# A two-layer hybrid RWKV / attention / Fourier block: the tile framework's scheduler with another machine model

## The chip, the core and the metric

The kernel runs on one core of one Trainium2 chip. The metric is the device time of one execution, in microseconds (us). The core has a matrix engine (PE, with its weight loads shown apart as PEld), a vector engine (DVE), a scalar engine (ACT), a general engine (POOL) and an engine that only issues transfers here (SP). Each engine takes its instructions strictly in the order that the built program gives it, and waits on semaphores for the others.

## The reference, cut to what matters

Two layers; 512 latent tokens and 256 context tokens, width 1024.

```python
for l in range(DEPTH):                       # 2 layers, the second without the context's output
    a  = modulate(rms_norm(h, ...), m[0], m[1]);  ac = the same for the context
    u  = a @ w_in[l]                         # one projection for three mixers and their gates
    # 1. RWKV-7, both directions, a state of 64x64 per head:
    #    S = S*w_t + (S @ -kk_t) b_t + v_t k_t ;  y_t = S r_t      (context first, then latent)
    # 2. windowed attention with the context as extra keys      3. 2-D Fourier mixing
    mix = (g_r*(y_r@wb_r) + g_a*(y_a@wb_a) + g_f*(y_f@wb_f)) @ w_out
    h   = h + m[2]*rms_norm(mix)
    h   = h + m[5]*rms_norm(conv_ffn(modulate(rms_norm(h), m[3], m[4])))
```

All matrix products are in float32 precision; the kernel makes each of three products of a rounded high part and a low rest.

## The kernel before, in words

**Products.** `gemm3` (lines 171 to 179) makes a product of 128-row blocks: for each block of the contraction three matmuls, on lines 177 (high by high), 178 (high by low) and 179 (low by high). A moving operand is 512 columns wide (latent tokens) or 256 (context tokens); in the ConvFFN of layer 0 it is 384. Weights come by `wload`: a transfer, a rounding on ACT (line 106) and the rest on POOL or DVE (line 118, `wl`).

**Stages of a layer.** First the projections that the RWKV mixer needs (`mix`, columns `COLS`). Then the RWKV chain: the tokens are cut into six windows of 128 (two of the context, four of the latent stream), each window into two chunks of 64, forward and backward direction together. For each window `wkv_features` makes decays, keys and products (matmuls on lines 814 and 864, DVE on 825 to 870), `wkv_inverse` inverts triangular blocks (matmuls 938 to 974, DVE 917 to 977), and for each chunk `wkv_prep` transposes (lines 987 and 997) and `wkv_step` advances the state (matmuls 1021 to 1052). One chunk needs the state of the chunk before: this is a chain over twelve steps, called the chain below. `rwkv_readout` follows (lines 1081 to 1107). Then Fourier mixing (lines 1298, 1305), attention (1222 to 1268), merging, the output projection, and the ConvFFN (`ffn`, the accumulation of its second product on line 604).

**What lies beside the chain.** The chain stands in blocks `with tc.high_priority()`. Beside it the kernel writes products that don't depend on it: eight column blocks for attention and Fourier (tile `stg`) and, by the generator `fill`, twelve blocks of gate columns (`AHEAD = 12`, written to `gd` through `sg`). Their accumulators have the PSUM tag `mm`. After that `self.banks(...)` hands the PSUM banks on, and the gates that are left take the tag `x`: they can't begin ahead of the chain's last use of its banks. These matmuls on lines 177 to 179 ahead of that point are called the fillers here.

**What sets the order.** No order is written out: the tile framework records the instructions of `run` in program order, each with its dependencies and a priority (program order, the high-priority blocks first). On leaving `tile.TileContext` (line 1804) its scheduler plays the program on a model of the machine: an engine that falls free in that model takes the ready instruction of the highest priority. The row in which the model took them is the order that stands in the program for each engine, for good. The model decides nothing else: which instructions there are, their operands and buffers' depth are the kernel's.

## Time and profile before

| | |
|---|---|
| time, median of 3 runs | 2510.15 us (2508.0 to 2512.45) |
| the profiled execution's own time | 2513.85 us |
| its span on the core | 2511.9 us, 43604 instructions |
| PE busy / PEld busy | 91% / 77% of the span |
| DVE / ACT / POOL busy | 75% / 42% / 38% |
| mean granted PE clock | 0.965 |

Busy time is the union of an engine's instructions. A matmul's shown duration reaches to the modelled end of its way through the array, and the next one starts long before that; how dense a stretch is shows in the distance of starts. The granted clock is a share of full speed: 1.0 is 2.4 GHz, 0.5 is 1.2 GHz, values between are means over a stretch. Lines are those of the kernel before. By the trace the stages of layer 0 are: projections up to about 148 us, the chain from there to 439, its readout to 473, Fourier mixing to 548, attention and merging to about 880, ConvFFN to about 1440; in layer 1 the chain runs from 1539 to 1812, its readout to 1833, and the ConvFFN from about 2135 to the end.

### The profile page before, as it was taken

The page shows a single profiled execution, that of the slowest core. Times are in us where ns is not written, and L with a number is a line of the kernel's source. Part 1 is how long each engine was busy: PE and PEld are TensorE (multiplying, and loading weights), DVE is VectorE, ACT ScalarE, POOL GpSimd, SP SyncE. Part 2 cuts the span into 40 slices and gives each one's busy share as a digit, 9 for nine tenths or more (in the row PEclk, how much of TensorE's full clock was granted, in tenths as well). Part 3 has the DMA queues.
Part 4 walks back from the last instruction along what each step waited for, and adds up shares of the span by engine and source line. Part 5 has one row for each costly group of instructions (what it writes and reads, how often), then busy time and mean ns, then how long its engine had stood idle before and what let it go on. Part 6 is the DMA issues. An engine that isn't in the chain of part 4 may idle for free. (4 is left out here: it accounts for less than half of the span.)

```text
span 2511.9 us, 43604 instructions
## 1 busy us (share of the span) xinstructions
PE 2293.3 (91%) x16612; PEld 1923.1 (77%) x16612; DVE 1889.0 (75%) x3458; ACT 1052.8 (42%) x2153; POOL 965.1 (38%) x965
## 2 busy tenths in 40 slices
PE   7878999999999979999999989889889997899997
PEld 4757777887777768898898777667667776888886
DVE  4967777838866587778778854888667857989988
ACT  3234343335434444343333544435345434544443
POOL 4443322023332363333333544343224424644453
PEclk9989989999999989999999999899999998999999
DMA  7611111644334322222222322112275643322321
GB/s 241 190 51 47 57 37 46 204 146 122 118 122 125 104 67 65 63 72 68 64 69 66 122 93 63 54 59 61 76 211 149 195 128 113 117 88 85 98 89 59
DMA packets 284529, 251.36 MB, mean 100 GB/s; under 512 B 14524, under 2 KB 241300, under 8 KB 284320
## 3 DMA queue, kind: packets, MB, share of 16 engines
q1 hardware_dynamic: 284320, 248.58, 32.0%
q8 instruction: 131, 2.15, 0.4%
q14 instruction: 78, 0.64, 0.1%
HBM read 221.23 MB, written 27.29 MB: 99 GB/s over the span
## 5 line engine op out<-in xcount | busy, mean ns | idle before, releaser
L177 PE MATMUL mm<-at,wh 128*128 128x256 f32 (+2 forms) x1968 | 661.8, 337 | 14.4 <-DVE v L614 7.0
L178 PE MATMUL mm<-at,wh 128*128 128x256 f32 (+2 forms) x1968 | 660.5, 336 | 12.8 <-POOL at L118 7.3
L179 PE MATMUL mm<-at,wl 128*128 128x256 f32 (+2 forms) x1968 | 659.7, 336 | 8.2 <-DVE wl L118 5.9
L118 POOL TENSOR_TENSOR wl<-wr,wh 128x512 fp32r<-128x512 f32 (+1 forms) x248 | 341.8, 1385 | 466.2 <-ACT wh L106 444.0
L177 PEld LDWEIGHTS mm<-at,wh 128*128 128x128 f32 x1968 | 380.8, 194 | 46.9 <-issue 5.6
L178 PEld LDWEIGHTS mm<-at,wh 128*128 128x128 f32 x1968 | 381.1, 194 | 43.4 <-POOL at L118 10.0
L179 PEld LDWEIGHTS mm<-at,wl 128*128 128x128 f32 x1968 | 380.9, 194 | 34.4 <-DVE wl L118 8.9
L106 ACT ACTIVATE wh<-wr 128x512 fp32r<-128x512 f32 (+1 forms) x342 | 204.9, 605 | 235.2 <-PE mm L178 141.3
L118 DVE TENSOR_TENSOR wl<-ws,wh 128x512 fp32r<-128x512 f32 x176 | 166.8, 949 | 65.6 <-ACT wh L106 65.6
L177 PE MATMUL x<-dh,hid 128*128 128x512 f32 x440 | 178.0, 405 | 29.8 <-DVE acc L604 27.7
L295 DVE SCALAR_TENSOR_TENSOR ma<-mw,s,ma 128x256 f32<-128x256 f32 x336 | 187.3, 597 | 11.0 <-DMA mw<-in_mod_w 8.2
L179 PE MATMUL x<-dh,hid 128*128 128x512 f32 x440 | 173.3, 395 | 1.0 <-DVE hid L118 1.0
L178 PE MATMUL x<-dl,hid 128*128 128x512 f32 x440 | 173.2, 394 | 0.0
L604 DVE TENSOR_TENSOR acc<-x,acc 128x512 f32<-128x512 f32 x200 | 134.4, 682 | 24.2 <-PE x L179 23.7
L118 POOL TENSOR_TENSOR dl<-dr,dh 128x1024 fp32r<-128x1024 f32 x44 | 112.2, 2549 | 83.9 <-ACT dh L106 83.9
L106 ACT ACTIVATE wh<-ws 128x512 fp32r<-128x512 f32 x170 | 103.7, 623 | 84.9 <-PE mm L178 70.5
L177 PEld LDWEIGHTS x<-dh,hid 128*128 128x128 f32 x440 | 83.3, 189 | 56.4 <-DVE acc L604 38.6
L154 POOL TENSOR_TENSOR ws<-wr,wr 128x512 f32<-128x512 f32 x42 | 66.4, 1580 | 139.5 <-DVE wl L118 136.9
L178 PE MATMUL x<-at,wh 128*128 128x512 f32 (+2 forms) x312 | 114.4, 367 | 5.0 <-POOL at L118 3.1
L177 PE MATMUL x<-at,wh 128*128 128x512 f32 (+2 forms) x312 | 114.7, 368 | 0.9 <-DVE wh L114 0.7
L106 ACT ACTIVATE P<-P,st 128x513 f32<-128x513 f32 (+5 forms) x120 | 86.0, 722 | 69.8 <-DVE P L1234 58.6
L154 POOL TENSOR_TENSOR ws<-ws,wr 128x512 f32<-128x512 f32 x42 | 62.8, 1495 | 132.5 <-DVE wl L118 75.0
(490 smaller groups left out, 4859.0 us busy)
## 6 DMA issues: line engine op xcount, KB each, us to landing
mw<-in_mod_w SPq DMA_DIRECT2D x96, 512.0 KB, 4.1
wr<-in_ffn_up SPq DMA_DIRECT2D x176, 256.0 KB, 3.1
wr<-in_w_in SPq DMA_DIRECT2D x164, 256.0 KB, 3.0
dr<-in_ffn_down SPq DMA_DIRECT2D x44, 512.0 KB, 3.3
gd<-sg SPq DMA_DIRECT2D x32, 256.0 KB, 2.0
wraw<-in_w_out SPq DMA_DIRECT2D x32, 256.0 KB, 3.7
hd<-h SPq DMA_DIRECT2D x32, 256.0 KB, 2.4
h<-hd SPq DMA_DIRECT2D x28, 256.0 KB, 6.7
```

Of the source, the lines that this page charges most:

```text
L106: return self.nc.scalar.activation(out, in_, func, **kw)
L118: e.tensor_tensor(lo, full, hi.bitcast(F32), ALU.subtract)
L154: e.tensor_tensor(raw[m], raw[x], raw[y], op)
L177: mm(ps, lhsT=lh, rhs=rh, start=first and k == 0, stop=False)
L178: mm(ps, lhsT=lh, rhs=rl, start=False, stop=False)
L179: mm(ps, lhsT=ll, rhs=rh, start=False, stop=last and k == nk - 1)
L295: nc.vector.scalar_tensor_tensor(acc[s], mw[:, k % 4], v, acc[s], ALU.mult, ALU.add)
L604: nc.vector.tensor_tensor(acc[i][:, cs], ps, acc[i][:, cs], ALU.add)
```

## The change

One argument. The scheduler plays the program on the framework's timeline simulator and no longer on its simple machine model.

```diff
-    with tile.TileContext(nc) as tc:
+    with tile.TileContext(nc, schedule_with_timeline_sim=True) as tc:
         Kern(tc, I, out).run()
```

The instructions are the same on PE (13680), DVE, POOL and SP; ACT has three table loads fewer. Their order differs on all five engines. Three places follow, each in the program before and in the changed one. In a row the tiles carry their buffer numbers: `x_588` is the PSUM tile of an inverse, `mm_...` the accumulator of a filler, `y_...` that of a step.

PE, layer 0, at the inverse of the chain's fourth window (line 938 is its first matmul). Before:

```order
L178 MATMUL mm_760_4834<-at_70_289,wh_754_4799 128x256
L179 MATMUL mm_760_4834<-at_69_288,wl_755_4800 128x256
L938 MATMUL x_588_3521<-iv_586_3517,MR_491_2911 32x16 x32
L177 MATMUL mm_760_4834<-at_71_290,wh_754_4799 128x256
L178 MATMUL mm_760_4834<-at_72_291,wh_754_4799 128x256
L179 MATMUL mm_760_4834<-at_71_290,wl_755_4800 128x256
L177 MATMUL mm_760_4834<-at_73_292,wh_757_4805 128x256
L178 MATMUL mm_760_4834<-at_74_293,wh_757_4805 128x256
L179 MATMUL mm_760_4834<-at_73_292,wl_758_4806 128x256
L944 MATMUL x_588_3521<-Ps_587_3520,TTt_585_3516 32x16 x16
L948 MATMUL x_588_3521<-TTt_585_3516,Ps_587_3520 16x16 x32
```

The same place in the changed program:

```order
L864 MATMUL x_578_3463<-W11_567_3414,BK_575_3442 128x128 x4
L938 MATMUL x_588_3521<-iv_586_3517,MR_491_2911 32x16 x32
L944 MATMUL x_588_3521<-Ps_587_3520,TTt_585_3516 32x16 x16
L948 MATMUL x_588_3521<-TTt_585_3516,Ps_587_3520 16x16 x32
L967 MATMUL x_590_3610<-iv_586_3517,MR_491_2911 32x32 x16
L987 MATMUL x_591_3647<-ident_2_61,vs__502_2950 128x128 x2
L987 MATMUL x_591_3647<-ident_2_61,vs__515_3008 128x128 x2
L974 MATMUL x_590_3610<-TTt_585_3516,Pb_589_3609 32x32 x16
```

The fillers that stood between the chain's matmuls here now stand ahead of this place. Counted from the start of the program, the fillers ahead of a point of the chain on PE are:

| point of the chain (layer 0: first four rows) | before | changed |
|---|---|---|
| first matmul of the first window's features (line 814) | 451 | 605 |
| first matmul of the first inverse (line 938) | 605 | 916 |
| first matmul of the fourth step (line 1021, `y_488`) | 732 | 1392 |
| last step (`y_697`) | 1111 | 1392 |
| layer 1: first inverse | 5829 | 6000 |
| layer 1: third step (`y_3206`) | 5879 | 6168 |
| layer 1: last step | 6168 | 6168 |

PE, layer 1, at the inverse of the chain's fourth window. Before:

```order
L864 MATMUL x_3307_17356<-W11_3296_17307,BK_3304_17335 128x128 x4
L178 MATMUL mm_3504_18758<-at_2843_14637,wh_3499_18748 128x512
L179 MATMUL mm_3504_18758<-at_2842_14636,wl_3500_18749 128x512
L177 MATMUL mm_3504_18758<-at_2844_14638,wh_3502_18754 128x512
L938 MATMUL x_3317_17414<-iv_3315_17410,MR_3220_16804 32x16 x32
L178 MATMUL mm_3504_18758<-at_2845_14639,wh_3502_18754 128x512
L179 MATMUL mm_3504_18758<-at_2844_14638,wl_3503_18755 128x512
```

The changed program:

```order
L814 MATMUL x_3297_17310<-xa_2911_14906,a2_2905_14883 128x128 x2
L864 MATMUL x_3306_17349<-W10_3295_17306,BK_3304_17335 128x128 x4
L864 MATMUL x_3307_17356<-W11_3296_17307,BK_3304_17335 128x128 x4
L938 MATMUL x_3317_17414<-iv_3315_17410,MR_3220_16804 32x16 x32
L944 MATMUL x_3317_17414<-Ps_3316_17413,TTt_3314_17409 32x16 x16
L948 MATMUL x_3317_17414<-TTt_3314_17409,Ps_3316_17413 16x16 x32
```

Here too the fillers are gone from between the chain's matmuls.

PE, ConvFFN of layer 0, where the second product of one group of columns (tiles `x_...`, from `dh`, `dl` and `hid`) meets the first product of the next (tiles `mm_...`). Before:

```order
L179 MATMUL x_2107_11121<-dh_2065_10919,hid_2064_10907 128x512
L177 MATMUL x_2108_11129<-dh_2027_10752,hid_2025_10739 128x512
L178 MATMUL x_2108_11129<-dl_2028_10753,hid_2025_10739 128x512
L179 MATMUL x_2108_11129<-dh_2027_10752,hid_2026_10740 128x512
L177 MATMUL x_2108_11129<-dh_2065_10919,hid_2063_10906 128x512
```

The changed program:

```order
L179 MATMUL x_2107_11121<-dh_2065_10919,hid_2064_10907 128x512
L178 MATMUL mm_2122_11192<-at_1676_9306,wh_2079_10955 128x384
L179 MATMUL mm_2122_11192<-at_1675_9305,wl_2080_10956 128x384
L177 MATMUL mm_2122_11192<-at_1677_9309,wh_2079_10955 128x384
L178 MATMUL mm_2122_11192<-at_1678_9310,wh_2079_10955 128x384
L177 MATMUL x_2108_11129<-dh_2027_10752,hid_2025_10739 128x512
```

Six matmuls of one second product were followed by six of the next; now four of a first product stand between them. In the ConvFFN of layer 1 the order on PE is unchanged.

## Rows read from the trace of the kernel before

**Rows 1.** The page's first lines: span, busy time of each engine.
```profile
span 2511.9 us, 43604 instructions
PE 2293.3 (91%) x16612; PEld 1923.1 (77%) x16612; DVE 1889.0 (75%) x3458; ACT 1052.8 (42%) x2153; POOL 965.1 (38%) x965
```
**Rows 2.** Busy time by stretch; columns: start:end, length, engines, granted clock, DMA share, GB/s.
```profile
147.60:212.40 64.80, 46.57 (x253) 40.30 (x253) 50.54 (x98) 24.62 (x57) 29.11 (x44) 0.84 0.14 46
212.40:278.00 65.60, 59.88 (x915) 47.27 (x916) 49.35 (x131) 30.05 (x79) 24.52 (x44) 0.95 0.14 44
278.00:438.80 160.80, 150.44 (x2111) 122.28 (x2111) 117.61 (x288) 63.41 (x163) 46.10 (x86) 0.94 0.15 46
438.80:473.50 34.70, 34.00 (x210) 25.43 (x209) 27.67 (x60) 15.58 (x21) 0.10 (x1) 1.00 0.69 223
473.50:548.00 74.50, 74.28 (x424) 64.98 (x424) 42.67 (x100) 20.76 (x37) 11.96 (x12) 0.98 0.53 161
1538.90:1643.60 104.70, 89.59 (x703) 72.39 (x702) 76.26 (x173) 47.32 (x109) 37.99 (x59) 0.85 0.18 56
1643.60:1812.00 168.40, 155.24 (x2300) 118.16 (x2299) 141.81 (x345) 76.01 (x191) 58.06 (x104) 0.98 0.19 60
1812.00:1833.50 21.50, 16.05 (x106) 8.98 (x106) 11.00 (x22) 10.27 (x15) 1.31 (x2) 1.00 0.66 215
```
**Rows 3.** The matmuls of line 177 alone, same stretches: length, PE, PEld, clock, DMA.
```profile
147.60:212.40 64.80, 18.73 (x52) 9.96 (x51) 0.84 0.14 46
212.40:278.00 65.60, 16.51 (x42) 8.31 (x42) 0.95 0.14 44
...
473.50:548.00 74.50, 36.33 (x104) 20.18 (x104) 0.98 0.53 161
1538.90:1643.60 104.70, 29.92 (x74) 15.07 (x74) 0.85 0.18 56
```
**Rows 4.** Timeline, fillers on PE: start, duration; 512 and 256 columns.
```profile
194.51 0.39 PE L177 MATMUL mm<-at,wh 128*128 128x512 f32 x1
...
194.74 0.39 PE L178 MATMUL mm<-at,wh 128*128 128x512 f32 x1
...
195.31 0.28 PE L178 MATMUL mm<-at,wh 128*128 128x256 f32 x1
...
195.43 0.28 PE L179 MATMUL mm<-at,wl 128*128 128x256 f32 x1
```
**Rows 5.** Timeline, the chain's own matmuls in the window 1735.1 to 1775.1.
```profile
1749.75 0.69 PE L1047 MATMUL y<-W,ZV 128*64 128x64 f32 x16
1750.36 0.68 PE L1052 MATMUL y<-MR,XV 64*64 64x64 f32 x16
...
1772.36 2.02 PE L864 MATMUL x<-W,BK 128*128 128x128 f32 x16 [1.31 <-DVE BK L855]
```
**Rows 6.** Who waited for whom, PE alone, 147 to 280 us: total, times, longest.
```profile
PE x L864 <- DVE BK L855: 9.8, 4, 4.1
...
PE x L864 <- DVE BK L854: 3.6, 1, 3.6
```
**Rows 7.** Busy time by stretch, single windows of the chain; columns as in Rows 2.
```profile
312.60:354.60 42.00, 37.79 (x538) 30.41 (x538) 33.61 (x84) 18.13 (x49) 14.35 (x29) 0.96 0.14 45
354.60:401.80 47.20, 42.99 (x532) 34.70 (x533) 34.26 (x85) 18.27 (x49) 14.31 (x29) 0.82 0.12 35
...
1735.10:1775.10 40.00, 37.53 (x523) 28.82 (x524) 35.34 (x87) 19.98 (x52) 14.73 (x29) 1.00 0.20 61
1775.10:1812.00 36.90, 35.54 (x753) 26.59 (x753) 24.19 (x70) 14.33 (x35) 7.39 (x12) 1.00 0.18 54
```
**Rows 8.** DVE's work for the fillers, 278.0 to 438.8: busy, mean ns | idle before.
```profile
L118 DVE TENSOR_TENSOR wl<-wr,wh 128x512 fp32r<-128x512 f32 x16 | 11.3, 705 | 8.3 <-ACT wh L106 8.2
```
**Rows 9.** The same for layer 1, 1643.6 to 1812.0.
```profile
L118 DVE TENSOR_TENSOR wl<-wr,wh 128x512 fp32r<-128x512 f32 x21 | 14.8, 709 | 1.1 <-PE mm L179 0.5 <-issue 0.5
```
**Rows 10.** Who waited for whom, PE alone, ConvFFN of layer 0 (942 to 1381 us).
```profile
PE x L177 <- DVE acc L604: 10.9, 9, 1.3
```

## The prediction

> **What bounds the kernel now.** I read first the busy times of the whole [rows 1]: PE is shown busy for 91% of the span, and nothing else comes near. Then the distance of starts of two fillers that follow each other [rows 4]: 194.51 to 194.74 is 0.23 us at 512 columns, 195.31 to 195.43 is 0.12 us at 256, although each is shown as 0.39 or 0.28 us long. So PE has more room than its busy share says, and where it lies is read by stretches [rows 2]. From 473.5 to 548.0 PE is busy for 74.28 of 74.50 us. Along the chain it holds far less: from 147.6 to 278.0 us (130.4 us) it carries 52 + 42 = 94 matmuls of line 177 [rows 3], so with lines 178 and 179 some 282 fillers, about 49 us at the distances above. In layer 1's 1538.9 to 1643.6 it is 74 × 3 = 222. Along the chain PE waits for DVE: early in layer 0 the feature products on line 864 stand at PE's head until `BK` is there, 9.8 and 3.6 us [rows 6].
>
> The window from 1735.1 to 1775.1 in layer 1 shows the chain's own pace [rows 7]: 40.0 us, of which DVE is busy for 35.34, that is 0.88, at full clock. So the two chains (291 us and 273 us long) are bound by DVE where fillers are few, and by a mixture of fillers ahead in PE's order, stalls of PE and DVE where they are many. The order decides how the two overlap, and it is what the change replaces.
>
> **The change, stretch by stretch.** The lists of the two programs tell the direction: in the changed one the fillers come early. In layer 0, 1392 − 451 = 941 of them stand between 147.6 us's place and the fourth step, where 281 stood; from there to the last step none is left, where 379 stood. In layer 1 it is 511 ahead of the third step, then none.
>
> *Layer 0, front.* The 941 fillers are 461 of 512 columns and 480 of 256: 461 × 0.23 + 480 × 0.12 = 164 us. The chain's matmuls come on top: a cluster of 16 small ones starts 0.61 us after the cluster before, a set of 16 feature products is 2.02 us long [rows 5]; a window has some 20 such clusters and sets, about 16 us, and 2.6 windows lie ahead of the fourth step: 42 us; at the least 0, if all of it fell into stalls of the fillers. Sum 206 us. How much PE stalls beside this I bound by 0.3% (74.28 of 74.50) and 28% (46.57 of 64.80, the stretch 147.6 to 212.4) [rows 2], and take 4%, nearer to the dense one since fillers now fill what was a stall: 214 us. Before, the fourth step came after 130.4 us. So **+84 us** at this point. The stalls of 9.8 and 3.6 us are in that: they go, and next late is PE itself, which the chain now waits for.
>
> *Layer 0, rest of the chain.* Before, it took 160.8 us with DVE busy for 117.61 [rows 2], of which 11.3 us were the fillers' low parts [rows 8]. Without them 106.3 us are left; at 0.88 that is 120 us, and 8 us more because the last window has no features to make beside it (24.19 busy of 36.90 us [rows 7]): 128 us. The readout's 34.70 us holds 27.67 of DVE; it takes in the Fourier products in the new order, I take 30 us, between 27.7 and 40. Together 158 against 195.5: **−37 us**.
>
> *Layer 0, after the readout.* Before, 74.5 us followed with 104 × 3 = 312 fillers and the Fourier products. Now 148 fillers are left, 76 × 0.23 + 72 × 0.12 = 26 us, and of Fourier, which now stands within the readout, I leave 3 us: 29 us, **−45 us**. If Fourier is not hidden there it costs up to 17 us more, the rest of the 74.5 us beside 312 × 0.175 = 55. Layer 0 in all: **+2 us**, between −25 and +35.
>
> *Layer 1.* The front has 511 fillers, 463 × 0.23 + 48 × 0.12 = 112 us, with 42 us of the chain 154, with 4% stalls 160 us, against 104.7: **+56 us**. The rest had 168.4 us with 141.81 of DVE, less 14.8 for fillers [rows 9]: 127.0 / 0.88 = 144, with the 8 us of the last window 152, and the readout's 21.5 unchanged: 173 against 189.9, **−17 us**. Here nothing is given back behind the readout, for before too all 6168 fillers were done by the last step. Layer 1: **+39 us**, between +10 and +60.
>
> *ConvFFN of layer 0.* PE waited 10.9 us for DVE to clear a PSUM bank (line 604) [rows 10]. Four matmuls of 384 columns between two second products give DVE that time. I take −6 us, ends −11 and +5. In layer 1's ConvFFN PE's order is the same: 0, ends −5 and +5, as ACT and DVE differ by a place or two. Attention differs throughout and no row favours a side: 0, ends −10 and +10. Three table loads fewer on ACT, which is busy for 42%: 0, ends −4 and 0.
>
> Sum: +2 + 39 − 6 = +35 us on the profiled execution's 2513.85 us: 2549. That execution lay 3.7 us above the median of 2510.15, so on the median's scale **2545 us**.
>
> **Two rules of the Trainium skill.** The 104 matmuls of line 177 from 473.5 to 548.0 are shown as 36.33 us, 349 ns each [rows 3], while they start 0.12 or 0.23 us apart. The Trainium skill (Trainium Kernel Development and Optimization, Performance Expectations) says that matmul busy time is a bad metric because matmuls are pipelined; by this the trace agrees. By busy time the 941 fillers would be priced at 328 us in place of 164, and the change would look 160 us worse in layer 0 alone; the sum above uses the distances.
>
> The clock falls where PE has little to do: 0.84 from 147.6 to 212.4 and 0.85 from 1538.9 to 1643.6, 0.98 in the dense stretch [rows 2]. The Trainium skill (TensorE: Matmul & The Clock Gate, Part 1: The HAM clock gate) says that half rate is the array's default and activity releases it. By that rule the emptied rest of the chain would run at a lower clock and the front at a higher one; the second rival prices this from rows.
>
> **The rivals.** *First, faster: the emptied chain lets DVE run without gaps.* For it: 35.34 of 40.0 us still contains waits on PE behind fillers, and these go. Against it: the chain's latency through PE and ACT stays. Place: the rest of the chain in both layers. At a DVE share of 0.95 and a front without stalls, layer 0 gives 206 − 130.4 = +76, then 106.3 / 0.95 + 4 + 28 = 144 (−51) and −45, so −20; layer 1 +49 and 127.0 / 0.95 + 4 + 21.5 = 159 (−31), so +18; the ConvFFN −11. In all −13: 2497 us. It decides from a share of about 0.93 on.
>
> *Second, slower still: the clock.* Without fillers PE may spend the rest of the chain at 1.2 GHz for much of the time. Two neighbouring windows with like DVE work (33.61 and 34.26) took 42.0 us at 0.96 and 47.2 at 0.82 [rows 7]: 5.2 us for one window. Against it: the two differ in more than the clock. Over the seven windows that are emptied it is 7 × 5.2 = 36 us: 2581 us.
>
> *Third, no change.* The front's loss of +84 and +56 is paid back if the chain of layer 1 has as much to win as that of layer 0; at a DVE share near 0.92 the sum is 2510 ± 5. That the argument does nothing is out: the lists differ.
>
> **How the numbers follow.** About 0.2% (5 us) is what a measurement of this kernel can tell from no change. Forecast, slower by about 35 us: 0.45. Clock, slower by about 70: 0.20. Faster by about 13 or, with attention and the ConvFFNs at their good ends, 25: 0.21. Within 5 us: 0.14. So faster 0.21, same 0.14, slower 0.65. The range 2490 to 2585 us leaves out the better half of the faster case and the clock at more than its price.
>
> **What would show each step.** Right: fillers dense on PE until the fourth step (which comes near 360 us) and the third step of layer 1 (near 1700 us, shifted by what layer 0 moved), then stretches with no line 177 at all, PE busy below 0.7 and DVE busy near 0.88; the Fourier products inside the readout; fewer waits of line 177 for line 604 in the first ConvFFN. Wrong: the front stalls on weights that ACT, POOL or DVE make late (the fillers' `wh` and `wl` keep their rank on those engines, which the lists can't price); a window of the emptied chain far from 36 us; or a gain in attention of more than 10 us, which no row here bounds well.

## The result

| | before | changed | ratio, 95% interval |
|---|---|---|---|
| time, median | 2511.3 us (2508.0 to 2514.08, 4 runs) | 2611.43 us (2611.03 to 2614.76, 4 runs) | 1.0402 (1.0384 to 1.0420) |
| span of the profiled execution | 2511.9 us | 2612.9 us | |
| mean granted PE clock | 0.965 | 0.919 | |

Slower, as forecast, but by 100 us and not by 35, and outside the range. The busy times answer to [rows 1]: DVE, ACT and POOL work as long as before to within 10 us, so on them the 101 us of the span are idle time; PE is shown busy for 26 us more. The first lines of the changed kernel's page, and its row of the granted clock in 40 slices of 65 us:

```profile
span 2612.9 us, 43644 instructions
PE 2319.4 (89%) x16612; PEld 1986.7 (76%) x16612; DVE 1889.6 (72%) x3458; ACT 1043.2 (40%) x2150; POOL 972.7 (37%) x965
...
PEclk9999976679999989999999899976689998999999
```

The two places with 6 and 7 are the emptied ends of the two chains. Where the time came in is seen from events that both traces have (starts, by the timelines; fillers are counted in PE's order):

| event | before | changed | shift | in this stretch | forecast |
|---|---|---|---|---|---|
| layer 0, step 4 of the chain | 278.0 | 350.8 | +72.7 | +72.7 | +84 |
| readout's end | 473.5 | 549.0 | +75.5 | +2.8 | −37 |
| filler 1540 | 550.2 | 609.0 | +58.7 | −16.8 | −45 |
| last product with `w_out` | 875.7 | 921.6 | +45.9 | −12.8 | 0 |
| ConvFFN's last sum (line 604) | 1447.5 | 1481.4 | +33.9 | −12.0 | −6 |
| layer 1, step 3 of the chain | 1643.6 | 1724.4 | +80.8 | +46.9 | +56 |
| readout's end | 1833.4 | 1939.6 | +106.2 | +25.4 | −17 |
| last product with `w_out` | 2096.5 | 2201.3 | +104.8 | −1.4 | 0 |
| end | 2511.9 | 2612.9 | +101.0 | −3.8 | 0 |

Three stretches miss the forecast by 40, 28 and 42 us, all to the slow side; the others lie 44 us to the fast side of it, so part of the misses cancels in the total. The stretches of the changed kernel, with the columns of [rows 2]: front, rest, readout and what follows in layer 0, then front, rest and readout in layer 1.

```profile
162.10:350.80 188.70, 184.03 (x1679) 158.94 (x1679) 118.03 (x260) 76.14 (x179) 51.49 (x80) 0.99 0.27 83
350.80:510.10 159.30, 103.23 (x1730) 89.19 (x1730) 99.18 (x261) 43.83 (x124) 40.16 (x80) 0.61 0.06 19
510.10:549.00 38.90, 31.98 (x161) 22.10 (x162) 26.73 (x60) 12.96 (x18) 0.30 (x3) 0.83 0.30 95
549.00:609.00 60.00, 41.55 (x216) 36.31 (x215) 44.75 (x106) 16.67 (x29) 7.90 (x8) 0.74 0.56 169
...
1592.00:1724.40 132.40, 128.46 (x902) 105.29 (x900) 92.93 (x194) 59.48 (x131) 39.96 (x48) 0.97 0.37 112
1724.40:1912.40 188.00, 115.17 (x2010) 99.19 (x2011) 124.91 (x323) 56.23 (x158) 48.91 (x102) 0.64 0.02 4
1912.40:1939.60 27.20, 21.43 (x112) 13.03 (x113) 14.67 (x31) 9.32 (x13) 0.10 (x1) 0.75 0.52 171
```

The fronts are dense, as the forecast had it (PE 184.03 of 188.70 and 128.46 of 132.40 us). The rests hold less work on every engine than before and are not shorter: in layer 0 PE has 103 us of work where it had 150, DVE 99 where it had 118, and the stretch takes 159.30 us where it took 160.80 [rows 2]. No engine is full there: DVE's share is 0.62 and not 0.88. One window of the emptied rest:

```profile
398.20:446.20 48.00, 30.12 (x450) 26.04 (x450) 31.09 (x80) 14.82 (x43) 13.62 (x29) 0.61 0.01 2
```

It takes 48 us, where 36 were forecast. Three things could make it so: PE's clock, the new order of the chain's own instructions, or a chain that was never bound by DVE's work. The experiments begin there. Times of an experiment are compared with runs of the kernel before on the same chip. Between the chips used that kernel's median lies at 2507.44 to 2511.88 us, so a difference between two experiments can be off by some 4 us. Lines in an experiment's rows are those of its own code, a few further down than in the kernel before.

### The profile page after: what moved, and what is told of

Same layout as the page of the kernel before. It is cut to its first block, busy times and chain, and to the rows that moved or that the text cites. A ratio compares the mean times of both kernels' runs of the same rounds, so it can differ in the third digit from the quotient of the medians.

```text
span 2612.9 us, 43644 instructions
## 1 busy us (share of the span) xinstructions
PE 2319.4 (89%) x16612; PEld 1986.7 (76%) x16612; DVE 1889.6 (72%) x3458; ACT 1043.2 (40%) x2150; POOL 972.7 (37%) x965
## 5 line engine op out<-in xcount | busy, mean ns | idle before, releaser
L177 PE MATMUL mm<-at,wh 128*128 128x256 f32 (+2 forms) x1968 | 650.0, 332 | 11.8 <-DVE wh L114 3.6
L179 PE MATMUL mm<-at,wl 128*128 128x256 f32 (+2 forms) x1968 | 645.5, 329 | 12.2 <-DVE wl L118 8.6
L178 PE MATMUL mm<-at,wh 128*128 128x256 f32 (+2 forms) x1968 | 646.2, 329 | 5.4 <-DVE at L118 5.1
L177 PEld LDWEIGHTS mm<-at,wh 128*128 128x128 f32 x1968 | 375.9, 191 | 45.0 <-issue 8.2
L178 PEld LDWEIGHTS mm<-at,wh 128*128 128x128 f32 x1968 | 376.3, 191 | 36.0 <-DVE at L118 6.3
L118 DVE TENSOR_TENSOR wl<-ws,wh 128x512 fp32r<-128x512 f32 x176 | 161.2, 920 | 26.5 <-ACT wh L106 25.3
L604 DVE TENSOR_TENSOR acc<-x,acc 128x512 f32<-128x512 f32 x200 | 132.8, 680 | 17.1 <-PE x L179 16.8
L864 PE MATMUL x<-W,BK 128*128 128x128 f32 (+1 forms) x384 | 74.0, 368 | 62.8 <-DVE BK L854 54.2
L154 POOL TENSOR_TENSOR ws<-wr,wr 128x512 f32<-128x512 f32 x42 | 75.2, 1791 | 126.3 <-DVE wl L118 125.1
L864 PEld LDWEIGHTS x<-W,BK 128*128 128x128 f32 x384 | 68.7, 274 | 67.4 <-issue 47.8
L177 PE MATMUL x<-at,wh 128*128 128x512 f32 (+2 forms) x312 | 115.2, 370 | 3.4 <-DVE mg L1429 1.6
```

What stands on the lines that cost most here:

```text
L118: e.tensor_tensor(lo, full, hi.bitcast(F32), ALU.subtract)
L154: e.tensor_tensor(raw[m], raw[x], raw[y], op)
L177: mm(ps, lhsT=lh, rhs=rh, start=first and k == 0, stop=False)
L178: mm(ps, lhsT=lh, rhs=rl, start=False, stop=False)
L179: mm(ps, lhsT=ll, rhs=rh, start=False, stop=last and k == nk - 1)
L604: nc.vector.tensor_tensor(acc[i][:, cs], ps, acc[i][:, cs], ALU.add)
```

## The experiments

### Fillers placed otherwise, clock, and the old scheduler without fillers

**b_ahead0 and b_early: the old scheduler's chain without fillers.**

```diff
-AHEAD = 12
+AHEAD = 0
```

> The kernel before with AHEAD = 0: no gate projection is issued along the chain, so that the old scheduler's chain runs without fillers from about the seventh step of layer 0 on (816 of 816 placed) and from the fifth of layer 1, while the front stays as before. Only the length of the windows is asked; the 1152 moved fillers lengthen the part behind. Theory A, an emptied window is slow whoever orders it: 45 to 49 us a window at a granted clock of 0.6 to 0.7. Theory B, the new scheduler's order of the chain is at fault: 36 to 41 us a window here.

```diff
         work = fill()
-        with tc.high_priority():
+        for _ in range(AHEAD):
+            self.advance(work, 1)
+        with contextlib.nullcontext():
             for w in range(2, 7):
...
         for _ in range(AHEAD):
-            self.advance(work, 1)
             self.advance(bg, MODS[l][0])
```

> The kernel before, with its scheduler, but the 12 gate projections are traced ahead of the chain's later windows and these windows have no raised priority: the list of PE then has all 1392 fillers of layer 0 ahead of the third step and all of layer 1 ahead of its third step. Theory A, the early fillers are the whole loss: the front of layer 0 ends near 360 us, the emptied windows take 45 to 50 us as in the changed kernel, and the time is 2580 to 2640 us. Theory B, it needs the new scheduler's order within the chain too: the emptied windows take 36 to 41 us under the old order, and the time is 2520 to 2560 us.

Beside the place of the fillers, b_early takes the raised priority from the chain's later windows and the readout; b_ahead0 keeps it. Measured: b_ahead0 2667.39 us (ratio 1.0622, 1.0586 to 1.0658), b_early 2701.45 us (1.0758, 1.0726 to 1.0790), above both of its theories. An emptied window of b_early, and its whole stretch from step 4 to step 12 in layer 0 and in layer 1; then that stretch of layer 1 in b_ahead0:

```profile
450.60:494.70 44.10, 30.31 (x448) 26.11 (x448) 32.31 (x80) 14.71 (x43) 13.97 (x28) 0.61 0.01 1
...
407.20:560.60 153.40, 104.72 (x1728) 89.94 (x1729) 106.14 (x268) 46.66 (x131) 41.80 (x82) 0.62 0.05 17
...
1840.70:1994.20 153.50, 101.57 (x1704) 87.33 (x1705) 108.34 (x274) 47.26 (x132) 43.73 (x89) 0.63 0.01 2
```

```profile
1738.90:1893.20 154.30, 103.71 (x1705) 89.19 (x1705) 107.66 (x272) 46.79 (x131) 42.76 (x87) 0.61 0.01 2
```

The windows lie between the theories: 42.2 to 44.7 us under the old order, at a clock of 0.58 to 0.69, where the new order takes 46.0 to 49.8 at 0.60 to 0.66. So some 4 us of a window are the new order. The rest is not. In layer 0 the kernel before drives 379 fillers through the stretch from step 4 to step 12 in 160.8 us; b_early, with none, takes 153.4: net of everything else, 7.4 / 379 = 0.02 us for a filler. In layer 1 the emptied stretch is even the longer one: 153.5 us in b_early and 154.3 in b_ahead0, where the kernel before takes 142.1 with 254 fillers in it (its row stands under pair_fine). In the front a filler costs its price: b_early's third step comes 122.5 us later for 718 more fillers ahead of it, 0.17 us each. So in the rest of the chain the fillers were all but free in sum, and their DVE work with them; to take them out gives nothing back.

This is a net number. Without the fillers the clock in layer 1's stretch is 0.61 to 0.63 and not 1.00, and the chain's own instructions stand in a slightly different order; what the fillers cost and what the higher clock gives back beside them is not parted here.

**warm4 and gap: the clock.** Both add matmuls without use to the emptied windows.

```diff
+    def warm(self, ps):
+        for _ in range(4 if self.dum is not None else 0):
+            self.nc.tensor.matmul(ps[:, :512], lhsT=self.dum[:, :128], rhs=self.dum[:, :512], start=True, stop=True)
...
         cc = self.ps("y")
+        self.warm(cc)
```

> The changed kernel with 448 matmuls of 128x512 added that compute nothing that is used: four ahead of the real ones into each PSUM tile of the chain's windows from the fourth window's features on, in both layers, 64 a window, about 15 us at 0.23 us each. They take no DVE time and no other engine waits for them but PE itself. Theory A, the clock: the emptied windows take 47 us because PE runs at 1.2 GHz there. Then the granted clock in them rises to 0.9 or more, a window falls to 38 to 41 us, and the kernel to about 2611 - 7 x 8 = 2555 us. Theory B, the hand-overs: the windows are as long as the chain through DVE, ACT and PE with its gaps, whatever the clock. Then the clock rises too, but a window stays at 45 to 50 us and the time at 2600 to 2640 us.

> The changed kernel with matmuls that compute nothing that is used, in the emptied windows of both layers, set where PE waits anyway: 5 of 128x512 ahead of the feature products of each direction, and directly behind the small clusters of the step and of the inverse 4 to 6 of 128 or 256 columns, in a free part of the same bank; about 9 us of PE a window. It asks again for the clock's part, without the four matmuls ahead of each cluster that stood in the chain's own way in warm4. Theory A, the clock: at a granted clock of 0.85 or more a window falls from 47 to 40 to 43 us, seven windows, 2570 to 2590 us. Theory B, the hand-overs between DVE, PE and ACT in the new order, whatever the clock: 46 to 49 us a window, 2605 to 2630 us.

Measured: 2647.87 us (1.0544, 1.0504 to 1.0584) and 2645.5 us (1.0543, 1.0507 to 1.0579). One window of warm4, then one of gap:

```profile
405.10:459.10 54.00, 41.79 (x513) 31.56 (x512) 31.41 (x80) 14.67 (x43) 13.41 (x28) 0.87 0.01 1
```

```profile
400.20:453.10 52.90, 38.72 (x496) 32.98 (x496) 31.32 (x80) 14.76 (x43) 13.55 (x29) 0.65 0.01 1
```

In warm4 the clock rose from 0.61 to 0.87 and the window grew from 48 to 54 us. That is no answer on the clock: the added matmuls, 15 us a window, stand in the chain's own way, and the window grew by 6 us only. In gap the clock hardly rose. Both times lie above their theories, and both runs are inconclusive on the clock's price.

What the clock costs PE itself can be read. In the emptied window of the changed kernel, in a piece at a clock of 0.50, two clusters of 16 matmuls start 1.04 us apart; at full clock the same two lines start 0.61 us apart [rows 5].

```profile
404.04 1.12 PE L1047 MATMUL y<-W,ZV 128*64 128x64 f32 x16 [1.05 <-DVE ZV L1042]
405.08 1.12 PE L1052 MATMUL y<-MR,XV 64*64 64x64 f32 x16
```

All of the chain's matmuls fill 30.12 us of that window; counted without the fillers, they fill 19.9 us of the window from 1735.1 to 1775.1 in the kernel before, at a clock of 1.00. So the low clock adds some 10 us to PE's work in a window. How much of it lengthens the window, and how much falls into PE's waits, no run separates.

**hold12: the fillers spread over the steps, under the new scheduler.**

```diff
+HOLD = (3, 3, 4, 5, 6, 6, 7, 8, 9, 9, 10, 11)
...
-            mm(ps, lhsT=lh, rhs=rh, start=first and k == 0, stop=False)
+            x = mm(ps, lhsT=lh, rhs=rh, start=first and k == 0, stop=False)
+            if k == 0 and self.hold is not None:
+                self.tc.add_manual_dep(x.ins, self.hold.name, ...)
...
+        self.steps.append(x.ins)
...
-        for _ in range(AHEAD):
+        for i in range(AHEAD):
+            self.hold = self.steps[HOLD[i]] if l in (0, 1) else None
             self.advance(work, 1)
+            self.hold = None
```

> The changed kernel with twelve order-only edges a layer: the first matmuls of each of the 12 gate projections may not stand on PE ahead of the first matmul of a given chain step (4, 4, 5, 6, 7, 7, 8, 9, 10, 10, 11, 12). Nothing else is asked of the scheduler. On PE's list the fillers ahead of the third to sixth window of layer 0 become 912, 1008, 1152, 1262, where 1392 stood ahead of all four. Theory A, the placement of the fillers alone is the loss: the windows fall back to 40 to 44 us, the last step of layer 0 comes near 440 to 455 us (510 in the changed kernel, 438.8 before), that of layer 1 falls by another 25 to 40, and the time is 2490 to 2540 us. Theory B, the new scheduler also orders the chain's own DVE and PE instructions worse: with fillers in them the windows stay at 46 us or more and the time stays above 2570 us.

Measured: 2629.06 us (1.0469, 1.0445 to 1.0493), slower than the changed kernel. Theory A, that their place alone is the loss, falls; theory B's windows and time came. The front was won back (step 4 at 299.1 us, 350.8 in the changed kernel), and the windows took it again: 63.3, 58.6 and 56.1 us. The timeline of PE shows how; the columns are start, duration, line, result and operands, size. Line 1027 is the step's first cluster, line 1035 its second, 180 to 185 are the fillers.

```profile
362.78 0.35 PE L1027 MATMUL y<-ZV,W 128*64 128x64 f32 x6
363.06 0.50 PE L180 MATMUL mm<-at,wh 128*128 128x512 f32 x1
...
365.08 0.63 PE L180 MATMUL mm<-at,wh 128*128 128x512 f32 x1
365.51 0.63 PE L184 MATMUL mm<-at,wh 128*128 128x512 f32 x1
...
369.13 0.40 PE L184 MATMUL mm<-at,wh 128*128 128x512 f32 x1
369.46 0.68 PE L1035 MATMUL y<-q,TTt 64*64 64x64 f32 x16
```

Twenty fillers stand between two clusters. All that the second cluster waits for is a copy of 0.42 us on DVE, which starts at 363.88, and it begins 6.4 us after the first of the fillers; in the trace of the kernel before 3 fillers stand at that place.

### The order of the features, and the size of the portions

**pair: both directions' products ahead of the first mask.** In the changed kernel DVE's timeline in the window shown above (idle time before an instruction and what ended it stand in brackets; line 869 is a mask, 726 to 854 the making of the second direction's `BK`):

```profile
410.01 0.68 DVE L869 TENSOR_TENSOR MR<-x,table 64x512 f32<-64x512 f32 x1 [4.21 <-PE x L864]
...
413.07 0.69 DVE L869 TENSOR_TENSOR MR<-x,table 64x512 f32<-64x512 f32 x1 [1.20 <-PE x L864]
...
415.18 0.29 DVE L726 TENSOR_SCALAR wt<-wt 128x256 f32<-128x256 f32 x1 [0.71 <-ACT wt L106]
...
420.17 0.85 DVE L854 TENSOR_TENSOR BK<-wt,wt 64x256 f32<-64x256 f32 x2
423.25 0.68 DVE L869 TENSOR_TENSOR MR<-x,table 64x512 f32<-64x512 f32 x1 [2.23 <-PE x L864]
```

DVE stands 4.21 us for PE's feature products of one direction, while the second direction's work, which would fill that time, comes behind.

```diff
+            W[d] = (W1, BK, vs, e1)
+        for d in range(2):
+            W1, BK, vs, e1 = W[d]
             for h in range(2):
                 ps = self.ps()
...
+                if d == 0 and h == 0:
+                    self.tc.add_manual_dep(x.ins, lastbk.ins.name, ...)
...
-            W[d] = (W1, BK, vs, e1)
```

> The changed kernel with the features of a window written in another order: the products of both directions are made on VectorE ahead of the first mask of either (one order-only edge a window holds the mask back). In the changed kernel's emptied windows VectorE stands 4.2 us before the first mask, with the second direction's products, 6.5 us of work, still to come; in b_early, under the old order, these overlap. Theory A, the new order within the chain costs 3 to 5 us a window: the stand of 4.2 us goes, the window falls from 47 to 43 us, twelve windows in the two layers, 2560 to 2585 us. Theory B, the order moves nothing, since the end of the window waits for the step and the inverse: 46 to 48 us and 2600 to 2620 us.

Measured: 2556.3 us (1.0191, 1.0170 to 1.0213), 55 us less than the changed kernel: theory A, and a little more than it said (2560 to 2585). An emptied window, and DVE's timeline in it (line 872 is the mask now):

```profile
425.80:464.30 38.50, 26.16 (x498) 22.20 (x498) 28.70 (x79) 10.26 (x30) 10.96 (x19) 0.67 0.01 1
```

```profile
439.00 0.68 DVE L872 TENSOR_TENSOR MR<-x,table 64x512 f32<-64x512 f32 x1 [3.21 <-PE x L867]
...
442.06 0.69 DVE L872 TENSOR_TENSOR MR<-x,table 64x512 f32<-64x512 f32 x1 [1.20 <-PE x L867]
...
443.40 0.67 DVE L872 TENSOR_TENSOR MR<-x,table 64x512 f32<-64x512 f32 x1
...
444.79 0.69 DVE L872 TENSOR_TENSOR MR<-x,table 64x512 f32<-64x512 f32 x1
```

The first stand has shrunk only from 4.21 to 3.21 (ahead of it PE itself waits 1.62 us for POOL, line 853), and a stand of 1.20 between the first masks is there in both, but there is one series of masks in place of two: the making of the second `BK` and its own stand of 2.23 no longer lie between. The window is 38.5 us long at a clock of 0.67, 2.5 us above the forecast's 36, which were taken from a window at full clock.

**b_pair_e: the same order under the old scheduler.** The edit of pair, in the kernel before.

> The kernel before, under its own scheduler, with the features in the order of pair. Its windows already make the second direction's products beside the first's feature products on PE (stands of 0.7 and 1.3 us at the masks). Theory A, the order is what the new scheduler lost and the old one had: nothing to win, 2505 to 2516 us. Theory B, the paired order is better in itself: 2 to 4 us a window, 2470 to 2495 us.

Measured: 2500.52 us (0.9972, 0.9957 to 0.9988). Seven us instead of 55: the old scheduler's list already had most of that overlap (in the window from 1735.1 to 1775.1 of the kernel before DVE stands 0.70 and 0.59 us at the masks). The time lies between the theories, nearer to A; the small rest is a gain.

**pair_hold: the edges of hold12 on top of pair.**

> The kernel of pair with the edges of hold12: the 12 gate projections of each layer spread over the steps 4 to 12. In hold12 the windows with fillers took 56 to 63 us, since the new scheduler sets 15 to 20 fillers in one lump between two clusters of a step (19 between lines 1021 and 1028, 6 us, where the kernel before has 3). Theory A, the lumps are the scheduler's own and come whatever the chain's order: windows of 50 to 58 us, 2560 to 2590 us. Theory B, the lumps came from the wait that pair removes: windows of 40 to 46 us, 2500 to 2535 us.

Measured: 2556.4 us (1.0199, 1.0167 to 1.0231), the time of pair. Step 4 of layer 0 came 43.3 us sooner than in pair, and the readout's end 2.7 us later: the fillers cost in the rest what they no longer cost in the front. The time lies just below theory A's; layer 0's windows took 47 to 54 us, layer 1's 42 to 49, so the lumps cost with the mended order too.

**pair_late: half of layer 0's gate projections held behind the chain.** As hold12 on pair, with `HOLD` holding six of the twelve behind the last step, in layer 0 alone.

> The kernel of pair with six of layer 0's gate projections (288 fillers, 150 to 180 per cent of what is left there now) held by order-only edges behind the chain's last step; layer 1 as in pair. Theory A: a filler in the front costs its price, 288 x 0.17 = 49 us, and behind the readout it is free as long as VectorE's 32 us of modulation products stand bare there (PE is busy for 41 of 60 us). Then the fourth step of layer 0 comes 25 to 45 us sooner than in pair (334.8), the stretch from the readout's end to filler 1540 grows by 25 to 35, and the time is 2530 to 2550 us. Theory B, fillers are worth the same wherever they stand: 2552 to 2560 us.

Measured: 2561.85 us (1.0227, 1.0198 to 1.0256); theory B. The fourth step came 18 us sooner, less than the 25 to 45 of theory A. The chain's last step came at 456.1 us instead of 484.1, but the readout, which the held fillers now stand in, took 63.0 us instead of 39.0.

**pair_fine: the fillers let go in small portions.** Each filler triple is held by an order-only edge behind one cluster of the chain, the triples spread evenly over the clusters of the windows.

```diff
+            if self.held is not None:
+                i, n = self.held
+                self.held = i + 1, n
+                self.tc.add_manual_dep(x.ins, self.marks[i * len(self.marks) // n].name, ...)
...
+        self.held = 0, AHEAD * KD * len(halves)
         for _ in range(AHEAD):
             self.advance(work, 1)
```

> The kernel of pair with finer order-only edges than pair_hold: along the windows 2 to 6, cluster by cluster of the chain (features, inverse, step; some 115 a layer), three to six fillers are let go behind each cluster on PE, where pair_hold let go 48 behind a step. On PE's list of layer 1 the 234 fillers from its fourth to its last step stand in 42 runs, 51 of them in runs of ten or more (pair_hold: 264 in 20 runs, 228; the kernel before: 254 in 56 runs, 72); in layer 0 it is 474 in 43, 308 in runs of ten or more. Theory A, it is the lump in one place that makes a filler cost its price in the chain: layer 1's stretch from the fourth to the last step falls from 169 us in pair_hold to 140 to 150 (142.1 in the kernel before, with 254 fillers), layer 0's gains less, and the time is 2515 to 2540 us. Theory B, under the new order a filler costs its price in whatever portions: layer 1's stretch stays at 160 to 172 us and the time at 2545 to 2560 us.

Measured: 2496.24 us (0.9942, 0.9921 to 0.9963): 60 us less than pair, better than theory A, and faster than the kernel before. Layer 1's stretch from the fourth to the last step, in the kernel before, the changed kernel, pair, pair_hold and pair_fine:

```profile
1670.70:1812.80 142.10, 132.28 (x1959) 101.38 (x1958) 119.52 (x296) 65.30 (x164) 50.08 (x91) 1.00 0.19 59
```

```profile
1752.40:1912.40 160.00, 99.57 (x1706) 86.00 (x1707) 102.35 (x261) 46.12 (x130) 42.08 (x87) 0.64 0.01 2
```

```profile
1711.90:1850.80 138.90, 95.50 (x1706) 81.23 (x1706) 100.88 (x261) 46.19 (x130) 42.19 (x87) 0.67 0.01 2
```

```profile
1682.30:1851.40 169.10, 143.46 (x1969) 117.18 (x1969) 114.09 (x281) 65.34 (x162) 44.93 (x88) 0.86 0.17 52
```

```profile
1652.40:1798.30 145.90, 128.94 (x1929) 100.57 (x1928) 110.68 (x278) 62.78 (x159) 45.91 (x90) 0.95 0.18 56
```

Read from the third row on: without fillers and with the chain's order mended 138.90 us; with 264 fillers in 20 portions 169.10, that is 0.11 us for each, half of the 0.23 between two starts; with 234 in 42 portions 145.90, 0.03 us each. The kernel before has 254 in 56 portions and 142.10. The same stretch of layer 0 in pair (129 fillers), pair_hold (528) and pair_fine (474):

```profile
334.80:484.10 149.30, 113.62 (x1858) 96.33 (x1858) 99.00 (x261) 49.68 (x133) 44.35 (x84) 0.75 0.12 38
```

```profile
291.50:483.10 191.60, 174.54 (x2248) 148.96 (x2248) 110.20 (x279) 66.70 (x167) 42.57 (x81) 0.88 0.17 51
```

```profile
295.10:455.40 160.30, 153.96 (x2197) 129.30 (x2196) 107.26 (x277) 64.54 (x163) 42.63 (x81) 0.99 0.19 58
```

Again a filler more than in pair costs 0.11 us in pair_hold and 0.03 in pair_fine. But here 308 of pair_fine's 474 stand in runs of ten or more, so the size of a portion is not the whole of it: the edges behind every cluster also change where in the chain the fillers stand, and the clock is higher. What the runs show is that fillers let go cluster by cluster cost nearly nothing net and fillers let go by whole projections do not; size and place are not parted.

**fine: the small portions alone, without pair's order.**

> The changed kernel with the fine edges of pair_fine and nothing else: the order of the features is the changed kernel's. Theory A, the two faults are of their own and add up: the lumps cost what pair_fine won over pair (2556 - 2496 = 60 us) and the order of the features what pair won over the changed kernel (55 us), so that this run lies near 2551 us, 2540 to 2565. Theory B, they are one: once fillers stand between the clusters in small portions, VectorE's stand at the masks is filled too or no longer decides, and the time is 2500 to 2525 us.

Measured: 2576.33 us (1.0269, 1.0249 to 1.0289). So the portions alone win 35 us over the changed kernel, the order alone 55, both 115. They are two faults, and the time lies above both theories, since the two together win more than the sum: with the one left in place, less of the other can be won, as layer 1's stretch shows, 171.6 us here with 234 fillers at a clock of 0.89, where pair_fine took 145.9.

**fine_late: four of layer 0's gate projections behind the chain.**

> The kernel of pair_fine with the last four of layer 0's twelve gate projections (192 fillers) held behind the chain, the first eight spread over its clusters; layer 1 as it is. On PE's list of layer 0 315 fillers then stand from the fourth to the last step, 108 in runs of ten or more (pair_fine: 474 and 308; the kernel before: 379 and 184). Theory A, the portions decide and the 32 us of modulation products behind the readout want cover: layer 0's stretch from the fourth to the last step falls from 160.3 us to 140 to 152, the 192 fillers lie beside the modulation products, and the time is 2475 to 2490 us. Theory B, what the stretch gains the fillers take back behind it: 2492 to 2502 us.

Measured: 2499.31 us (0.9958, 0.9944 to 0.9972). The stretch fell to 144.3 us (292.1 to 436.4), as theory A had it, and the readout grew from 35.1 to 50.0 us and took it back: theory B for the time.

### Behind the readout, and the ConvFFN

**mods_late: the modulation products moved on.**

```diff
-MODS = ((1, 0, 1), (0, 0, 2))
+MODS = ((0, 0, 2), (0, 0, 2))
```

> The changed kernel with MODS[0] = (0, 0, 2): the modulation products on VectorE (line 295, 32 us after the readout of layer 0) are asked for during attention alone and not beside the gate projections. Theory A, they are what takes the gain after the readout: with only 148 fillers left, PE (busy for 9.6 of 28 us) waits for VectorE. Then the 58 us from the readout's end to filler 1540 fall to 30 to 40, attention takes up to 10 of it back, and the time is 2585 to 2605 us. Theory B, attention's VectorE is as full as the stretch before it: nothing is gained, 2605 to 2625 us.

The changed kernel behind the readout of layer 0: its first 28 us by engine, DVE's largest group from 549 to 607 us, and PE's longest wait there.

```profile
549.00:577.00 28.00, 9.62 (x48) 8.27 (x46) 25.35 (x64) 6.37 (x10) 0.10 (x1) 0.59 0.51 155
```

```profile
L295 DVE SCALAR_TENSOR_TENSOR ma<-mw,s,ma 128x256 f32<-128x256 f32 x70 | 32.3, 519 | 0.4 <-DMA mw<-in_mod_w 0.3
```

```profile
PE x L311 <- DVE ma L295: 10.7, 3, 6.1
```

Measured: 2620.67 us (1.0442, 1.0417 to 1.0466). The stretch from the readout's end to filler 1540 fell from 60.0 to 26.7 us, near the forecast's 29, and PE is busy throughout it:

```profile
551.20:577.90 26.70, 26.70 (x153) 23.52 (x153) 3.19 (x6) 9.48 (x17) 7.54 (x7) 1.00 0.31 101
```

So the modulation products do take the gain there, as theory A had it; the time is theory B's. Attention gave all of the gain back (first product of the attention branch +62.0 us against the kernel before, +50.3 in the changed kernel): DVE has to do these 32 us somewhere, and in the kernel before they lay beside the 312 fillers that followed the readout.

**b_ffn3 and b_pair_ffn: the ConvFFN's second products spread, in the kernel before.**

```diff
-                if f > closed + 1 or step >= (5 if ctx else 6):
-                    m = 6 if ctx else 1
+                if f > closed + 1 or step >= (3 if ctx else 6):
+                    m = 3 if ctx else 1
```

> The kernel before, with one part of the new order alone: in layer 0's ConvFFN the second products are traced in groups of 3 behind the third to sixth first product, where they were traced 6 and 6 behind the last two. The waits of PE for VectorE to clear a bank (line 604, 10.9 us in the kernel before) are to go. Theory A, the spread of the second products is the 14 us that the changed kernel wins there: 2497 to 2506 us. Theory B, it is not, or hid is late when it is asked for sooner: 2510 to 2520 us.

> The kernel before with both edits, pair's order of the features and b_ffn3's spread of the second products. Theory A, they lie in different stretches and add up: the difference of b_pair_e to the kernel before, and 5 to 11 us less. Theory B, they do not: as b_pair_e.

Measured: b_ffn3 2502.72 us (0.9963, 0.9944 to 0.9982), with layer 0's ConvFFN ending 10.8 us sooner in the two traces; theory A. PE's wait of 10.9 us for line 604 [rows 10] is 0.6 there, and 1.0 in the changed kernel, in this row:

```profile
PE x L177 <- DVE acc L604: 1.0, 1, 1.0
```

b_pair_ffn: 2494.88 us (0.9953, 0.9935 to 0.9971). The two edits add up within the noise of their runs, and this kernel needs no change of the scheduler. It, pair_fine and fine_late are the fastest here; their intervals overlap.

## Why the prediction was right in direction and wrong in size

**Right: the direction, the two fronts, the ConvFFN.** The fronts cost +72.7 and +46.9 us where +84 and +56 were forecast; a filler in front of the chain costs its distance of starts, 0.17 us by b_early. The stalls at the feature products on line 864 went, and the rests hold no fillers, as said. The ConvFFN's gain was right in its mechanism and came to −12.0, just beyond its end of −11; the 10.9 us of waits at line 604 were nearly all of it, where I took half.

**Wrong: "106.3 us are left; at 0.88 that is 120 us", and the same in layer 1.** This is the step that failed. The rests were forecast at 128 and 152 us and took 159.3 and 188.0: 31 and 36 of the 40 and 42 us that the two places miss. (The other 9 and 6 are the readouts, 38.9 and 27.2 us for 30 and 21.5; the Fourier products stood in layer 0's for the most part, as said.) The step took the chain for bound by DVE's work, took the fillers' work off it, and divided the rest by a share of 0.88. But 0.88 was the share of one window with the fillers' DVE work in it, 4.4 of its 35.34 us:

```profile
L118 DVE TENSOR_TENSOR wl<-wr,wh 128x512 fp32r<-128x512 f32 x6 | 4.4, 730 | 0.3 <-issue 0.2
```

Without that work the window has 0.77, the whole rest of the kernel before (141.81 − 14.8) / 168.4 = 0.75 in layer 1 and (117.61 − 11.3) / 160.8 = 0.66 in layer 0 [rows 2, 8, 9], and the best emptied stretch, that of pair, has 100.88 / 138.90 = 0.73. The chain is a row of hand-overs between PE, DVE and ACT; fillers and their low parts lay in its gaps on both engines, at a net 0.02 us each in layer 0 and at less than nothing in layer 1 (b_early, b_ahead0). What was forecast to be given back by their leaving was never paid. This was in the rows: the share should have been formed after the subtraction, not before it.

The new order of the chain's own instructions came on top: pair won 10.0 us of layer 0's rest and readout and 20.5 of layer 1's, and 16 and 11 in the two fronts, though 129 and 81 fillers moved from its fronts into its rests. No term of the sum had it; the prediction looked at fillers among the chain's clusters and not at the chain among itself. This accounts for 20.5 of layer 1's 42 us and 10 of layer 0's 40. What is left, some 22 and 30 us, lies in the share, in the readouts and in the lower clock; the runs do not part the clock from the share.

**Wrong: −45 us behind the readout.** It was −16.8. The 29 us were worked out from PE's fillers alone; DVE's 32 us of modulation products, which stood in the same stretch before, were left without cover, and mods_late shows 26.7 us without them. What is late next there was not asked of DVE.

**The rivals.** The faster case fell with the DVE share. No change fell with it; besides, its 2510 at a share near 0.92 needs the first rival's front without stalls and its other terms, for with the forecast's own that share gives about 2535. The clock fell as the second rival said, to 0.61 and 0.64 over the rests. It is not what parts the changed kernel from pair, which goes through layer 1's emptied stretch in 138.90 us at 0.67 where the changed kernel takes 160.00 at 0.64. But that it costs nothing is not shown: PE's own work in a window grows by some 10 us, and under the old scheduler layer 1's stretch took 142.10 us at 1.00 with 254 fillers and 153.5 and 154.3 at 0.63 and 0.61 without. The 36 us that the rival put on seven windows would find room in what is left above. How much of the idle time that pair's window still has on DVE (38.5 − 28.7 = 9.8 us) is the clock and how much the hand-overs themselves stays open, for warm4 and gap put matmuls in the chain's way.

**What stays open.** Why the scheduler on its timeline simulator puts fillers in portions of twenty between two clusters, and masks ahead of the second direction's products, was not tried: that needs its assumed times beside the chip's. The runs show that these two things in its order cost time, and that both can be mended by order-only edges and, for the masks, another order of writing. The clock's price in an emptied chain, and the size of a portion against its place, stay open too.

## What to carry to other kernels

A chain of short hand-overs with an engine's share of 0.7 to 0.9 need not be bound by that engine, and was not here: take the other work's part off the share before it is used, and ask what the chain takes alone. Work that fills such a chain's gaps was nearly free where it was let go cluster by cluster, cost half to two thirds of its price in portions of some thirteen to eighteen (0.11 us for a filler in pair_hold) and its full price as a block ahead (0.17 us in layer 0's mixture), so a scheduler's list is read by the size and place of its portions and not by its counts. When work is moved away from a stretch, what is left there on the other engines loses its cover and has to be priced too.

## What the runs showed of the hardware

Two clusters of 16 small matmuls started 0.61 us apart at full clock and 1.04 us apart in an emptied window, at a granted clock of 0.50 there. Matmuls added to raise the clock did not pay for themselves: in warm4's window it was 0.87, in the changed kernel's 0.61, and the windows took 54.0 and 48.0 us. And the clock can fall in the middle of a dense run: in hold12's portion, after a stretch of small clusters and waits at 0.50 to 0.61, the fillers began at full clock and ran at 1.2 GHz from 364.0 to 367.4, 0.43 us between starts in place of 0.23 [rows 4], though PE was then never idle; behind it they ran at full clock again. The row of that piece:

```profile
364.00:367.40 3.40, 3.40 (x10) 2.63 (x9) 0.31 (x1) 0.00 (x0) 0.00 (x0) 0.51 0.00 0
```
